# Turning the products of c with the first w_ada columns round, in the prelude of a hybrid attention and retention layer

## The chip, the cores and the metric

The kernel runs on one core of one Trainium2 chip. Its engines are TensorE (PE in the profile, with its weight loads as PEld), VectorE (DVE), ScalarE (ACT), GpSimd (POOL) and SyncE (SP). Each engine works through its own instructions in order, and semaphores hold one engine back until another, or a DMA, has reached a certain point. DMAs are issued from SP, ACT and POOL. The metric is the time of one execution on the device in microseconds (us); lower is better.

## The reference, cut to what matters

All data is float32. The sequence has 512 rows, the model 2048 columns, and there is one layer.

```python
def hybrid_layer(x, c_act, g, w_ada, b_ada, w_in, w_out, dec_f, dec_b):
    mod = c_act @ w_ada + b_ada                      # c_act = silu(c), (1, 2048); w_ada (2048, 6144)
    shift, scale, gate = jnp.split(mod, 3, axis=-1)
    h = rms_norm(x, g) * (1.0 + scale[:, None]) + shift[:, None]
    proj = jnp.einsum('bsd,df->bsf', h, w_in)        # w_in (2048, 7168)
    ...                                              # dilated attention, retention, gates
    out = jnp.einsum('bsf,fd->bsd', y, w_out)
    return x + gate[:, None] * out
```

What the change touches is the first part: for the first 128 model columns (called k = 0 here), the shift and the scale, each a sum over 2048 rows of w_ada, and the first 128 columns of h, which every projection needs.

## The kernel before, in words

**Layout.** The projections want h with the model's columns on the partitions, in 16 pieces of 128 columns by 512 rows. x arrives with its rows on the partitions, in four tiles `xn[0]` to `xn[3]` of 128 rows by 2048 columns (named xt0 to xt3, or xt, in the profile). Each tile is squared and summed (`squares_a` on ACT for the left half, `squares` on DVE for the right half), the factor of the RMS norm is made (`factor`: a small DVE instruction, then a power on POOL), the tile is scaled on DVE (`scaled`), and its 16 blocks of 128 by 128 are transposed by TensorE (`k0_part` for the first block, `turned` for the other 15 in four banks of PSUM) and copied to SBUF (`evacuated`, on ACT or DVE). The first block of each tile stays in PSUM, in `psk` (tiles 0 to 2) and `psk3` (tile 3).

**Shift and scale of k = 0.** They come from two blocks of w_ada, 2048 rows by 128 columns each: `raw0[0]` (shift, raw00 in the order below) and `raw0[1]` (scale, raw01). Each is loaded in two halves of 512 KB (`load0(q, b, i)`: block b, half i), in 512-byte runs. `sums0(b, i)` makes the eight products of half i: before, the 128 by 128 piece of w_ada is the stationary operand and one column of silu(c) (`ct`) the moving one, so the sum lands with one number on each partition, in column b of `psa`. `turn_rows` transposes the row of biases and gains that was loaded from DRAM, and two DVE instructions copy it to `bg`. `shift_scale0` adds the biases and gives `sv` and `av`, and `h0_sum` and `h0_low` make h of k = 0 as a pair: `hh` (rounded) and `hl` (what the rounding left).

**After the prelude.** The projections run over groups of the 16 pieces of h (1, 2, 2, 3, 4 and 4 of them). For the first piece, all 13 first units of w_in (256 columns each) are multiplied with h of k = 0, each as three products (high by high, high by low, low by high). Meanwhile DVE sums the columns of w_ada for the next group (`aacc`, line 214), and splits the weights into high and low parts (`wlo`, line 540).

**What sets the order.** `pin` keeps an instruction at the place where the program text has it on its engine. Instructions without `pin`, among them the two copies of `turn_rows` on DVE, are placed by a scheduler. `warm(n, ps)` issues n products of two constant tiles whose result nobody reads; each product of 128 by 128 floats shows as two rows in the profile. Loads issued from SP and from ACT share eight semaphores, which the build hands out in turn (DMAHW0 to DMAHW7): a ninth load waits, on the engine that issues it, until the earlier load with the same semaphore has landed. On ACT the loads stand ahead of all of its other instructions.

## Time and profile before

| what | us |
|---|---|
| median of 3 runs | 975.18 (973.9 to 975.6) |
| the profiled execution's own time | 976.19 |
| span of its trace | 974.4 |
| PE busy in the span | 952.7 (98%) |
| DVE, ACT, POOL busy | 615.3, 375.4, 14.4 |
| first square of x on ACT (line 308) starts | 5.77 |
| first product with w_ada (line 294) starts | 16.04 |
| first h on ACT (line 364) starts | 37.17 |
| first projection product (line 90) starts | 38.24 |

Times in the trace count from the start of the span. The stretches in the table of windows give, for each engine, its busy time and its number of instructions, then the TensorE clock that was granted (1.00 is full speed), the mean busy share of the DMA engines and the bytes moved. The granted clock has its first record at 8.8 us; the 1.00 shown ahead of that is no measurement. TensorE ends are modelled, so the start-to-start distance of a run of products tells more than the length of one.

### The profile page before, as it was taken

How to read it: one execution, taken by the hardware profiler on the slowest of the kernel's cores; microseconds unless marked ns; L12 is line 12 of the kernel's file. 1: busy time of each engine (PE TensorE's matmuls, PEld its weight loads, DVE VectorE, ACT ScalarE, POOL GpSimd, SP SyncE). 2: the span in 40 equal slices, each digit the busy share in tenths (PEclk: the TensorE clock that was granted, in tenths of full speed). 3: DMA queues.
4: the chain of work that ended last, by engine and by line, in shares of the span. 5: the costliest groups of instructions: out<-in, count | busy, mean ns of one | idle time of the engine just before them, and what ended most of it. 6: DMA issues, size and time to landing. Idle time of an engine off the chain costs nothing.

```text
span 974.4 us, 14375 instructions
## 1 busy us (share of the span) xinstructions
PE 952.7 (98%) x5596; PEld 832.0 (85%) x5596; DVE 615.3 (63%) x1078; ACT 375.4 (39%) x735; POOL 14.4 (1%) x25
## 2 busy tenths in 40 slices
PE   6999899999999999999999999999999999999996
PEld 6887689787988888988998899998899988888896
DVE  4599999957968776664565556745534382535444
ACT  3554425234236554454343242422333372333321
POOL 2000000000000000000000000000000000000001
PEclk8699999999999999999999999999999999999999
DMA  9697889633552122212224625426313158234304
GB/s 330 197 327 234 281 263 325 207 106 109 186 181 78 54 87 65 66 44 87 67 86 143 204 66 184 141 80 202 124 55 98 54 167 284 87 118 141 109 1 173
DMA packets 108947, 141.49 MB, mean 145 GB/s; under 512 B 5656, under 2 KB 78024, under 8 KB 108496
## 3 DMA queue, kind: packets, MB, share of 16 engines
q1 hardware_dynamic: 107056, 135.57, 43.1%
q10 hardware_dynamic: 1728, 4.98, 1.3%
q8 instruction: 44, 0.72, 0.3%
q14 instruction: 23, 0.19, 0.1%
q0 software_dynamic: 96, 0.03, 0.0%
HBM read 136.36 MB, written 4.20 MB: 144 GB/s over the span
## 4 chain that ended last, share of the span: by engine, by line
PE 89%; DMA 4%; DVE 4%; issue 1%; ACT 0%; POOL 0%; SPq 0%; POOLq 0%; DVEq 0%; ACTq 0%
PE pp L92 24%; PE pw L92 15%; PE pp L90 12%; PE po L92 12%; PE pw L90 7%; PE po L90 6%; PE op L92 3%; PE sp L92 2%; DMA graw<-in_w_ada_dram 2%; PE op L90 2%; DMA raw<-in_w_ada_dram 1%; PE tp L774 1%; PE psa L294 1%; PE sp L90 1%; DVE aacc L214 1%
## 5 line engine op out<-in xcount | busy, mean ns | idle before, releaser
L539 ACT CAST whi<-raw 128x512 fp32r<-128x512 f32 (+1 forms) x289 | 175.0, 606 | 428.3 <-PE pp L92 198.1
L540 DVE TENSOR_TENSOR wlo<-raw,whi 128x512 fp32r<-128x512 f32 (+1 forms) x289 | 194.1, 672 | 213.2 <-ACT whi L539 206.6
L90 PE MATMUL pp<-whi,hh 128*128 128x256 f32 x576 | 162.4, 282 | 0.0
L92 PE MATMUL pp<-wlo,hh 128*128 128x256 f32 x576 | 161.8, 281 | 0.3 <-DVE wlo L540 0.3
L92 PE MATMUL pp<-whi,hl 128*128 128x256 f32 x576 | 161.4, 280 | 0.0
L90 PEld LDWEIGHTS pp<-whi,hh 128*128 128x128 f32 x576 | 108.4, 188 | 2.5 <-ACT sc L843 1.7
L92 PEld LDWEIGHTS pp<-wlo,hh 128*128 128x128 f32 x576 | 108.4, 188 | 1.5 <-DVE wlo L540 0.7
L92 PEld LDWEIGHTS pp<-whi,hl 128*128 128x128 f32 x576 | 108.4, 188 | 0.0
L90 PE MATMUL pw<-hh,whi 128*128 128x512 f32 x256 | 103.6, 405 | 3.3 <-DVE acc L946 1.8
L90 PE MATMUL pp<-hh,whi 128*128 128x512 f32 x256 | 101.8, 398 | 0.4 <-DVE kl L674 0.4
L92 PE MATMUL pw<-hh,wlo 128*128 128x512 f32 x256 | 102.1, 400 | 0.0
L92 PE MATMUL pp<-hh,wlo 128*128 128x512 f32 x256 | 101.5, 396 | 0.0
L92 PE MATMUL pw<-hl,whi 128*128 128x512 f32 x256 | 101.5, 397 | 0.0
L92 PE MATMUL pp<-hl,whi 128*128 128x512 f32 x256 | 101.1, 395 | 0.0
L92 PE MATMUL po<-wlo,yh 128*128 128x512 f32 (+1 forms) x252 | 92.6, 367 | 0.0
L90 PE MATMUL po<-whi,yh 128*128 128x512 f32 (+1 forms) x252 | 92.5, 367 | 0.0
L92 PE MATMUL po<-whi,yl 128*128 128x512 f32 (+1 forms) x252 | 92.5, 367 | 0.0
L214 DVE SCALAR_TENSOR_TENSOR aacc<-araw,ct,aacc 128x512 f32<-128x512 f32 (+2 forms) x75 | 76.1, 1015 | 4.1 <-ACT aacc L210 2.7
L946 DVE TENSOR_TENSOR acc<-acc,pw 128x512 f32<-128x512 f32 x100 | 66.9, 683 | 8.2 <-PE pw L92 7.8
L999 DVE SCALAR_TENSOR_TENSOR gacc<-graw,ct,gacc 128x512 f32<-128x512 f32 x60 | 45.0, 750 | 35.1 <-DMA graw<-in_w_ada_dram 34.4
L90 PEld LDWEIGHTS pw<-hh,whi 128*128 128x128 f32 x256 | 48.5, 190 | 18.7 <-DVE acc L946 4.8
L90 PEld LDWEIGHTS pp<-hh,whi 128*128 128x128 f32 x256 | 48.1, 188 | 13.6 <-ACT e L719 0.9
(230 smaller groups left out, 1586.1 us busy)
## 6 DMA issues: line engine op xcount, KB each, us to landing
raw<-in_w_in_dram SPq DMA_DIRECT2D x94, 512.0 KB, 3.6
araw<-in_w_ada_dram SPq DMA_DIRECT2D x48, 512.0 KB, 6.2
graw<-in_w_ada_dram SPq DMA_DIRECT2D x64, 256.0 KB, 2.8
raw<-in_w_out_dram SPq DMA_DIRECT2D x32, 512.0 KB, 3.8
raw<-in_w_in_dram SPq DMA_DIRECT2D x16, 384.0 KB, 4.0
araw<-in_w_ada_dram SPq DMA_DIRECT2D x16, 384.0 KB, 4.2
res<-in_x_dram SPq DMA_DIRECT2D x16, 256.0 KB, 6.0
raw<-in_w_in_dram SPq DMA_DIRECT2D x10, 256.0 KB, 4.1
```

Of the source, the lines that this page charges most:

```text
L90: nc.tensor.matmul(o, lh, rh, start=start, stop=False, skip_group_check=True)
L92: nc.tensor.matmul(o, a, b, start=False, stop=stop and b is (rl if swap else rh), skip_group_check=True)
L214: ins = nc.vector.scalar_tensor_tensor(acc[:, :, :n], rv[:, a], ct[:, kr + a : kr + a + 1], acc[:, :, :n], op0=ALU.mult, op1=ALU.add,)
L294: nc.tensor.matmul(psa[:, b : b + 1], raw0[b][:, a, :], ct[:, a : a + 1], start=a + b == 0, stop=a == NK - 1, skip_group_check=True,)
L539: c1 = nc.scalar.copy(dh, src)
L540: c2 = nc.vector.tensor_tensor(dl, src, f32(dh), op=ALU.subtract)
L774: nc.tensor.transpose(tp_[:, j * P : (j + 1) * P], pt[:, j * P : (j + 1) * P], ident)
L946: nc.vector.tensor_tensor(accs[u][i], accs[u][i], ps[i], op=ALU.add)
L999: nc.vector.scalar_tensor_tensor(st["acc"], raw, ct[:, kr : kr + 1], st["acc"], op0=ALU.mult, op1=ALU.add)
```

## The change

The operands of `sums0` are exchanged: one column of silu(c) is stationary, the 128 by 128 piece of w_ada moves, and the sum is a row of 128 numbers on partition 0 of `psa`. `sums0_turned` copies the two rows to SBUF on ACT and turns them into columns with two small transposes. Tile 1 of x is loaded from ACT's queue and not from SP's, so that the four halves of `raw0` follow directly on half of tile 0 on SP. `h0_sum` is divided: `h0_high` issues the ACT half, and columns 0 to 383 and 384 to 511 are made at different places. The order of the prelude and the counts of warming products are new.

```diff
-WARM = 8, 2, 4, 2
+WARM = 9, 2, 8, 6, 4
...
-    for q, t, a, b in ((nc.scalar, 0, 0, 1024), (nc.sync, 0, 1024, D), (nc.sync, 1, 0, D), (nc.scalar, 2, 0, D), (nc.scalar, 3, 0, D)):
+    for q, t, a, b in ((nc.scalar, 0, 0, 1024), (nc.sync, 0, 1024, D), (nc.scalar, 1, 0, D), (nc.scalar, 2, 0, D), (nc.scalar, 3, 0, D)):
         q.dma_start(xn[t][:, a:b], x2[t * P : (t + 1) * P, a:b])
...
-                    psa[:, b : b + 1], raw0[b][:, a, :], ct[:, a : a + 1],
+                    psa[0:1, b * P : (b + 1) * P], ct[:, a : a + 1], raw0[b][:, a, :],
...
+    def sums0_turned():
+        pin(nc.scalar.copy(row0, psa[0:1, 0 : 2 * P]))
+        for b in range(2):
+            pin(nc.tensor.transpose(psa[:, 256 + b : 257 + b], row0[:, b * P : (b + 1) * P], ident[0:1, 0:1]))
...
+    def h0_high(cols, src):
+        marks["hh"] = pin(nc.scalar.activation(hh[0][:, cols], src, AF.Identity, scale=av[:, 0:1], bias=sv[:, 0:1]))
+
     def h0_sum(cols, src):
-        a, b = av[:, 0:1], sv[:, 0:1]
-        marks["hh"] = pin(nc.scalar.activation(hh[0][:, cols], src, AF.Identity, scale=a, bias=b))
-        pin(nc.vector.tensor_scalar(tmp0[:, cols], src, a, b, op0=ALU.mult, op1=ALU.add))
+        pin(nc.vector.tensor_scalar(tmp0[:, cols], src, av[:, 0:1], sv[:, 0:1], op0=ALU.mult, op1=ALU.add))
...
-    evacuated(0, 0, act)
-    evacuated(0, 1, act)
+    for b in range(4):
+        evacuated(0, b, act)
+    warm(WARM[2], psk3)
+    sums0(0, 0)
+    turn_rows()
     squares_a(1)
     squares(1)
     factor(1)
-    squares_a(2)
-    squares(2)
-    factor(2)
...
+    scaled(1, 1024, D)
+    turned(1, 2)
+    turned(1, 3)
+    sums0(0, 1)
+    squares_a(2)
+    squares(2)
+    factor(2)
+    evacuated(1, 2, act)
+    evacuated(1, 3, act)
+    sums0(1, 1)
     scaled(2, 0, P)
     scaled(2, P, 1024)
+    sums0_turned()
     k0_part(2)
     turned(2, 0)
     turned(2, 1)
+    shift_scale0()
     squares_a(3)
     squares(3)
     factor(3)
-    scaled(1, 1024, D)
+    h0_sum(A, psk[:, A])
+    scaled(3, 0, P)
     scaled(2, 1024, D)
...
+    h0_high(A, psk[:, A])
+    turned(2, 2)
+    warm(WARM[3], ps0)
     k0_part(3)
+    warm(WARM[4], ps0)
+    h0_low(A)
+    marks["conv1"] = [marks["hh"], marks["hl"]]
+    h0_high(B, psk3[:, 0:P])
+    h0_sum(B, psk3[:, 0:P])
+    h0_low(B)
+    turned(2, 3)
```

Where instructions stand, with the semaphores that each waits for. First ACT's queue from the program's start. Before:

```order
L123 DMA xt0_110<-in_x_dram 128x1024
L123 DMA xt2_112<-in_x_dram 128x2048
L123 DMA xt3_113<-in_x_dram 128x2048
L129 DMA raw_122<-in_w_in_dram 128x512
L308 ACT_TABLE_LOAD
L308 ACTIVATE sqa_161,ssx_128<-xt0_110 128x1024 [waits DMAHW0_49]
```

With the change:

```order
L123 DMA xt0_110<-in_x_dram 128x1024
L123 DMA xt1_111<-in_x_dram 128x2048
L123 DMA xt2_112<-in_x_dram 128x2048
L123 DMA xt3_113<-in_x_dram 128x2048 [waits DMAHW0_49]
L129 DMA raw_122<-in_w_in_dram 128x512 [waits DMAHW4_49]
L315 ACT_TABLE_LOAD
L315 ACTIVATE sqa_163,ssx_128<-xt0_110 128x1024
```

ACT now issues five loads, and the last two of them wait: xt3 for the load that had DMAHW0 before it, and raw_122 (the first piece of w_in) for the load that had DMAHW4.

Which load has DMAHW4 is seen on TensorE, with the change, from the eight warming products behind tile 0 on (a product waits for the semaphore of the load it reads):

```order
L378 MATMUL psk3_150<-ident_130,ones_135 128x128 x8
L296 MATMUL psa_147<-raw00_108,ct_141 1x128 [waits DMAHW3_49]
L296 MATMUL psa_147<-raw00_108,ct_141 1x128 x7
L272 MATMUL ps0_149<-ident_130,bg_row_107 128x48 [waits DMASW2_49,DMASW1_49]
L339 MATMUL psk_148<-ident_130,xt1_111 128x128 [waits DMAHW2_49,DVE_49]
L347 MATMUL psx_234<-ident_130,xt1_111 128x128 [waits DVE_49,PE_49,Activation_49]
...
L296 MATMUL psa_147<-raw01_109,ct_141 1x128 [waits DMAHW4_49]
L296 MATMUL psa_147<-raw01_109,ct_141 1x128 x7
L347 MATMUL psx_255<-ident_130,xt1_111 128x128 [waits DVE_49,Activation_49]
```

DMAHW4 belongs to raw01_109, the first half of the scale's block; DMAHW0 (as in ACT's first square before) to the half of tile 0 that ACT loads. The biases' transposes (line 272) stand behind the first eight products on TensorE.

Last, VectorE between tile 0 and tile 1. Before:

```order
L326 TENSOR_SCALAR xt0_110<-xt0_110,rsx_129 128x1024
L313 ISA sqd_203,ssx_128<-xt1_111 128x1024 [waits DMAHW3_49]
L313 ISA ssx_128 128x1
L318 SCALAR_TENSOR_TENSOR ms1_205<-ssx_128 128x1 [waits DVE_49,Activation_49]
L313 ISA sqd_210,ssx_128<-xt2_112 128x1024 [waits DMAHW2_49]
L313 ISA ssx_128 128x1
L273 COPY bg_146<-ps0_149 128x48 [waits PE_49]
```

With the change:

```order
L333 TENSOR_SCALAR xt0_110<-xt0_110,rsx_129 128x1024
L273 COPY bg_146<-ps0_149 128x48 [waits PE_49]
L274 TENSOR_SCALAR bg_146<-bg_146 128x16 [waits DVE_49]
L320 ISA sqd_226,ssx_128<-xt1_111 128x1024 [waits DMAHW2_49]
L320 ISA ssx_128 128x1
L325 SCALAR_TENSOR_TENSOR ms1_228<-ssx_128 128x1 [waits DVE_49,Activation_49]
L333 TENSOR_SCALAR xt1_111<-xt1_111,rsx_129 128x128 [waits Pool_49]
```

The copy of the biases (line 273), which waits for TensorE's line 272, now stands ahead of the squares of tile 1; before, it stood behind the squares of tiles 1 and 2.

## The prediction

> **What bounds the kernel now.** I read the page's first part, then the table of windows over the first 58 us, then the timeline of each engine there. Over the whole span TensorE sets the time, so an edit in the prelude is worth what it moves the start of the projections, counted at full clock.

> ```profile
> PE 952.7 (98%) x5596; PEld 832.0 (85%) x5596; DVE 615.3 (63%) x1078; ACT 375.4 (39%) x735; POOL 14.4 (1%) x25
> ...
> 12.25:16.04 3.79, 0.00 (x0) 0.00 (x1) 3.62 (x11) 1.82 (x4) 2.42 (x2) 0.95 1.09 327
> 16.04:36.89 20.85, 20.85 (x101) 20.55 (x101) 5.91 (x13) 4.97 (x11) 1.28 (x1) 0.50 0.93 285
> 36.89:38.24 1.35, 0.00 (x0) 0.00 (x1) 0.61 (x3) 1.07 (x3) 0.00 (x0) 0.50 0.05 7
> 38.24:43.00 4.76, 4.76 (x13) 3.81 (x14) 4.72 (x10) 2.91 (x7) 0.00 (x0) 0.51 0.22 57
> 43.00:58.00 15.00, 15.00 (x86) 12.93 (x86) 11.70 (x22) 13.07 (x27) 0.00 (x0) 1.00 0.90 283
> ```

> TensorE is idle from 12.25 to 16.04; within that gap the clock falls to half, and it stays there through 20.85 us of unbroken one-column products and transposes, until 42.9, about 4.7 us after dense projection products began at 38.24. So what ends last ahead of the projections is TensorE itself, at half speed, behind a load.

> At full clock two projection products take 0.47 us:

> ```profile
> 45.53 0.47 PE pw L92 x2
> ...
> 40.11 1.05 PE L340 MATMUL psx<-ident,xt 128*128 128x128 f32 x4
> ```

> The 13 instructions of 38.24 to 43.00 are these four transposes and nine products, worth 9 x 0.235 + 4 x 0.13 = 2.6 us at full clock. The present start, at full clock, is thus 43.0 - 2.6 = 40.4. That is the number to beat.

> **The change, part by part.** It removes the half-speed one-column products and would keep the clock up; but it puts two waits into ACT's queue ahead of everything ACT does. Now that queue runs straight through:

> ```profile
> 0.74 1.38 ACTq L123 DMA_DIRECT2D xt<-in_x_dram  x3
> 2.15 1.09 ACTq L129 DMA_DIRECT2D raw<-in_w_in_dram  x1
> 3.27 1.28 ACT L308 ACT_TABLE_LOAD   x1 [3.27 <-issue]
> 5.57 1.23 DVE L313 CUSTOM_DVE_ANT_0 sqd<-xt 128x1024 f32<-128x1024 f32 x1 [4.69 <-DMA xt<-in_x_dram]
> 5.77 1.06 ACT L308 ACTIVATE sqa<-xt 128x1024 f32<-128x1024 f32 x1 [1.23 <-DMA xt<-in_x_dram]
> ```

> The table load follows 0.03 us behind the last DMA issue: they share one order. With the change the fifth issue waits for raw01's first half to land. Queued behind it are the table load, the squares of tile 0 and all copies from PSUM; DVE's factor waits for that square, POOL for the factor, TensorE for the scaled tile. **First term: when does that half land?** With x on ACT's queue (q10) and w_ada's 512-byte runs on SP's (q1) the windows of the DMA show:

> ```profile
> q10 hardware_dynamic: 109, 0.76, 93.2%
> q1 hardware_dynamic: 107, 0.05, 8.6%
> ...
> q1 hardware_dynamic: 1180, 0.60, 118.7%
> ...
> DMA to landing us min/median/max: 15.7/15.7/15.7
> ...
> 16.04 3.57 PE L294 MATMUL psa<-ct,raw 128*128 128x1 f32 x16 [3.83 <-DMA raw<-in_w_ada_dram]
> ```

> The first two are 10 to 12 us, the third 14 to 16, the fourth the one recorded landing among w_ada's four loads. The queues alternate packet by packet, so the queue with small packets gets 0.05 MB while x gets 0.76. Being issued first does not bring w_ada first. After tile 0 (5.57) three tiles of x, 3.15 MB, take 3.15 / 0.38 = 8.3 us, in which w_ada gets 0.2 MB; of the two pieces in question, 1.05 MB, 0.84 remain, at 0.30 MB/us 2.8 us: 16.7. Upper bound: before, the recorded landing fits only the second load, issued at about 2.1, thus 17.8 (the first was in use at 16.04), and the bytes ahead of it are nearly the same now. I take 17.3.

> Restart of ACT: an issue of 0.46 (three in 1.38) to 1.09, the table 1.28, so the first square starts at 19.1 (18.4 to 20.2) instead of 5.77. **Second term: tile 0.**

> ```profile
> 3.67 3.78 PE L372 MATMUL psk<-ident,ones 128*128 128x128 f32 x16 [3.67 <-POOL mln L145]
> 8.62 0.37 PE L332 MATMUL psk<-ident,xt 128*128 128x128 f32 x1
> 8.82 0.97 PE L340 MATMUL psx<-ident,xt 128*128 128x128 f32 x7
> 10.04 1.09 PE L340 MATMUL psx<-ident,xt 128*128 128x128 f32 x8 [0.25 <-DVE xt L326]
> 10.97 1.06 PE L372 MATMUL psk<-ident,ones 128*128 128x128 f32 x8
> 19.72 1.70 PE L340 MATMUL psx<-ident,xt 128*128 128x128 f32 x7
> ```

> The seven transposes came 3.05 us after the square: 22.1. TensorE has by then stood idle since about 8.5, far longer than the 3.8 us that halved its clock, so 15 transposes cost 3.2 (seven took 1.70 at half clock, 0.97 at full): 25.3. Eight warming products, 16 rows, take 3.4 as at the start of the trace: 28.8. Then the first eight products, 16 rows of the warming kind, as the new operands give: 3.4 at half clock, 1.9 at full. With the clock back 4.7 us after dense work began (25.3 + 4.7 = 30.0) they end at 31.2 (30.7 to 32.3).

> **Third term: tile 1, no longer covered.** Its squares and scaling ran from 10.93 to about 15 inside the wait for w_ada. Now DVE's copy of the biases stands ahead of them and waits for a transpose behind those products.

> ```profile
> 13.49 0.20 DVE L273 COPY bg<-ps 128x48 f32<-128x48 f32 x1
> 13.76 0.17 DVE L274 TENSOR_SCALAR bg<-bg 128x16 f32<-128x16 f32 x1
> 10.93 1.23 DVE L313 CUSTOM_DVE_ANT_0 sqd<-xt 128x1024 f32<-128x1024 f32 x1 [0.94 <-DMA xt<-in_x_dram]
> 12.27 0.16 DVE L318 SCALAR_TENSOR_TENSOR ms<-ssx 128x1 f32<-128x1 f32 x1
> 7.27 0.56 POOL L322 TENSOR_TENSOR rsx<-ms,mhalf 128x1 f32<-128x1 f32 x1 [3.57 <-DVE ms L318]
> 14.01 1.83 DVE L326 TENSOR_SCALAR xt<-xt,rsx 128x128 f32<-128x128 f32 x4
> ```

> Bias transpose and copies 0.8: 32.0. Squares to scaling 1.34 + 0.16 + 0.56 and two hand-overs, 2.15; two scalings 0.92: 35.1. TensorE then has 15 transposes (2.0) and 24 products (5.6) at full clock: 42.7. If the cover were still there this term would be nothing.

> **Fourth term: the tail.** The turn back (a PSUM copy on ACT, two transposes of one row, three small adds) is new. Nearest rows: a copy of 256 columns, three in 1.12; the adds from 36.25 to 37.13. I take 1.4, between 1.0 and 2.2: 44.1. Then DVE does tile 3's squares (1.5), the low part's product (0.68) and the scalings of tile 3's first block and tile 2's right half (0.28 + 0.74): 47.3. TensorE follows with four transposes, six and four warming products around one transpose, and four transposes: 20 rows at 0.13 and 9 at 0.13, 3.6. First projection at 50.9, on a full clock.

> ```profile
> 20.82 1.12 ACT L353 COPY xT<-psx 128x256 f32<-128x256 f32 x3 [6.75 <-PE psx L340]
> 36.25 0.15 DVE L301 TENSOR_TENSOR sv<-psa,bg 128x1 f32<-128x1 f32 x1
> 36.98 0.15 DVE L303 TENSOR_TENSOR av<-av,bg 128x1 f32<-128x1 f32 x1
> L365 DVE TENSOR_SCALAR ht<-psk,av,sv 128x384 f32<-128x384 f32 x1 | 0.7, 677 | 0.7 <-ACT hh L364 0.7
> SPq L563 <- DVE av L303: 10.6, 1, 10.6
> ...
> 19.55 6.87 SPq L203 DMA_DIRECT2D araw<-in_w_ada_dram  x6
> 37.09 5.10 SPq L563 DMA_DIRECT2D raw<-in_w_in_dram  x2
> ```

> The two earlier h parts hide under these steps and cost nothing. The pieces of w_ada for the next group wait for the buffers of the squares, which come later now; SP stood 10.6 us with nothing to issue, so that is covered too (up to 1 us if not).

> **Sum:** 50.9 - 40.4 = +10.5 us on the profiled 976.19, so 986.7; the median of the runs is 1.0 lower, so 985.7, and I say **986**.

> [...]

> **Rivals.**

> *The clock falls again (22%).* Between the first products and tile 1 TensorE is idle about 3 us, again about 2.5 between tile 2's transposes. Speaking for it: 3.8 us were enough before, and transposes did not restore it. Price: tile 1's 15 transposes and first products at half, until 4.7 us after these begin, +4.5; a second fall +4 more. 990 to 994.

> *w_ada gets more than packet for packet (8%).* If the queues shared time equally, 1.05 MB would need 7 us behind tile 0, landing near 13 and not 17.3: about 4 us off, 982. The 109 against 107 packets speak against it.

> *ACT is not held (10%): faster.* If the wait sits with the DMA and not with the engine, ACT starts as before, and the change does what it says. The first products start at 16.04 on a live clock: 17.9; biases 18.7; tile 1 21.8; TensorE's 7.6: 29.4; turn 30.8; DVE 34.0; projections at 37.6 instead of 40.4: -2.8, so 972. It is decided on ACT's first square: the eight products wait for 16.04 while tile 0 with its eight warming products is done at 10.97 + 2.1 = 13.1, so there are 2.9 us of slack, and the break-even is a first square near 5.8 + 2.9 + 2.8 = 11.5 us. For it stands only that the trace shows no such wait on ACT; against it the one order of issue and table load above, and SP's 10.6 us, a wait in which nothing behind it was issued. [...]

> **How the numbers follow.** The forecast, held until the landing and the clock back once, has 55% and its own range 982 to 989; the clock's second fall 22%, equal time 8%, ACT free 10%, and 5% for results between 973 and 981 by partial waits. The range 978 to 994 leaves out ACT free and the ends. About 0.2% (2 us) is what this measurement can tell from no change. Faster: nearly all of "ACT free", 9%. Same: 4%. Slower: 87%.

> **What would show it.** In the changed profile: ACT's first square (line 315) near 19 with a gap behind ACT's issue of w_in; granted clock 0.50 at 20 to 30; the first products with w_ada near 29, in rows of 0.12 after the clock's return; h on ACT near 45; the first projection near 51, then a trace like the old one shifted by ten. I am wrong if the first square starts before 11.5, if w_ada's second load lands before 13, or if the projections start before 43.

## The result and the profile after

The changed kernel takes 985.04 us (median; 984.71 to 986.82) against 974.91 for the kernel before beside it: a ratio of 1.0108, 95% interval 1.0091 to 1.0126. It is slower by 1.1%, as forecast (986, 978 to 994). The profiled execution took 985.0 us with a span of 983.2.

First the start of the changed kernel: its timeline up to the first projection product (start in us, duration in us, engine, line, operation, how many; in brackets the idle time before and what ended it).

```profile
17.18 0.33 ACTq L129 DMA_DIRECT2D raw<-in_w_in_dram  x1
17.54 1.28 ACT L315 ACT_TABLE_LOAD   x1 [17.54 <-DMA raw<-in_w_ada_dram]
18.84 1.06 ACT L315 ACTIVATE sqa<-xt 128x1024 f32<-128x1024 f32 x1
...
21.27 0.48 PE L339 MATMUL psk<-ident,xt 128*128 128x128 f32 x1 [12.74 <-DVE xt L333]
...
21.87 3.12 PE L347 MATMUL psx<-ident,xt 128*128 128x128 f32 x15
...
24.82 1.95 PE L378 MATMUL psk<-ident,ones 128*128 128x128 f32 x16
...
26.70 1.91 PE L296 MATMUL psa<-raw,ct 128*1 128x128 f32 x16
...
28.84 0.21 DVE L273 COPY bg<-ps 128x48 f32<-128x48 f32 x1 [5.79 <-PE ps L272]
...
29.16 1.22 DVE L320 CUSTOM_DVE_ANT_0 sqd<-xt 128x1024 f32<-128x1024 f32 x1
...
31.66 0.47 PE L339 MATMUL psk<-ident,xt 128*128 128x128 f32 x1 [2.86 <-DVE xt L333]
...
32.35 1.73 PE L347 MATMUL psx<-ident,xt 128*128 128x128 f32 x7 [0.21 <-DVE xt L333]
...
34.01 3.57 PE L296 MATMUL psa<-raw,ct 128*1 128x128 f32 x16
...
38.82 3.65 PE L296 MATMUL psa<-raw,ct 128*1 128x128 f32 x32
...
46.90 0.63 PE L347 MATMUL psx<-ident,xt 128*128 128x128 f32 x4 [2.67 <-DVE xt L333]
...
50.06 0.48 PE L90 MATMUL pw<-hh,whi 128*128 128x512 f32 x1
```

ACT did nothing until 17.54; what ended its wait was a load of w_ada, right behind its issue of the first piece of w_in (line 129). TensorE stood idle for 12.74 us ahead of tile 0's first transpose, and for 2.86 us more ahead of tile 1's. The same stretches in the table of windows of the changed kernel (busy time and instructions of PE, PEld, DVE, ACT and POOL, then the granted TensorE clock):

```profile
21.09:24.50 3.41, 3.11 (x14) 2.82 (x15) 1.89 (x6) 1.12 (x3) 0.00 (x0) 0.50 1.00 372
24.50:31.33 6.83, 4.30 (x37) 3.48 (x35) 1.69 (x6) 2.14 (x4) 0.55 (x1) 1.00 0.51 153
31.33:38.16 6.83, 6.29 (x27) 4.04 (x28) 3.72 (x8) 2.17 (x5) 0.55 (x1) 0.50 0.19 50
38.16:50.06 11.90, 8.78 (x79) 7.34 (x77) 5.48 (x14) 5.74 (x13) 0.55 (x1) 1.00 0.54 171
```

The clock came back at 24.50, was lost at 31.33 for 6.83 us, and came back at 38.16. The first projection product starts at 50.06 on a full clock. Against the old start counted at full clock, 40.4, that is 9.66 us; from the tenth to the 160th projection product the changed trace is in fact behind the old one by 9.64 to 9.69 us, but for twelve of them (10.1 to 11.2), and up to the 200th by 9.5 to 10.0. So an account of the prelude at full clock gives the shift of the products that follow. Later the changed trace makes up about 1 us (8.4 to 8.7 behind from the 350th product on), and the spans differ by 8.8.

### The profile page after: what moved, and what is told of

The parts are those of the page before. It is cut to its first block, busy times and chain, and to the rows that moved or that the text cites. A ratio compares the mean times of both kernels' runs of the same rounds, so it can differ in the third digit from the quotient of the medians.

```text
span 983.2 us, 14429 instructions
## 1 busy us (share of the span) xinstructions
PE 948.1 (96%) x5624; PEld 824.5 (84%) x5624; DVE 613.9 (62%) x1076; ACT 376.3 (38%) x738; POOL 12.3 (1%) x25
## 4 chain that ended last, share of the span: by engine, by line
PE 87%; DMA 5%; DVE 4%; issue 2%; ACT 1%; POOL 0%; SPq 0%; POOLq 0%; DVEq 0%; ACTq 0%
PE pp L92 24%; PE pw L92 14%; PE pp L90 12%; PE po L92 12%; PE pw L90 7%; PE po L90 6%; PE op L92 3%; PE sp L92 2%; DMA graw<-in_w_ada_dram 2%; DMA raw<-in_w_ada_dram 2%; PE op L90 2%; PE tp L783 1%; DVE aacc L214 1%; PE sp L90 1%; DMA araw<-in_w_ada_dram 1%
## 5 line engine op out<-in xcount | busy, mean ns | idle before, releaser
L92 PE MATMUL pp<-wlo,hh 128*128 128x256 f32 x576 | 161.8, 281 | 0.6 <-DVE wlo L549 0.6
L92 PE MATMUL pp<-whi,hl 128*128 128x256 f32 x576 | 161.3, 280 | 0.0
L92 PEld LDWEIGHTS pp<-wlo,hh 128*128 128x128 f32 x576 | 108.4, 188 | 1.7 <-DVE wlo L549 0.8
L92 PEld LDWEIGHTS pp<-whi,hl 128*128 128x128 f32 x576 | 108.4, 188 | 0.0
L92 PE MATMUL pw<-hh,wlo 128*128 128x512 f32 x256 | 101.4, 397 | 0.0
L92 PE MATMUL pp<-hh,wlo 128*128 128x512 f32 x256 | 101.3, 396 | 0.0
L92 PE MATMUL pw<-hl,whi 128*128 128x512 f32 x256 | 101.1, 395 | 0.0
L92 PE MATMUL pp<-hl,whi 128*128 128x512 f32 x256 | 100.9, 394 | 0.0
L92 PE MATMUL po<-wlo,yh 128*128 128x512 f32 (+1 forms) x252 | 92.6, 367 | 0.0
L92 PE MATMUL po<-whi,yl 128*128 128x512 f32 (+1 forms) x252 | 92.5, 367 | 0.0
```

What stands on the lines that cost most here:

```text
L92: nc.tensor.matmul(o, a, b, start=False, stop=stop and b is (rl if swap else rh), skip_group_check=True)
```

## The experiments

My theory: ACT's queue, held until the first half of the scale's block has landed, makes the loss; what comes behind it (tile 1 uncovered, the clock) sets its size. The rivals: the loss sits in the exchanged operands and their turn back, in the uncovered tile 1, or in the clock alone. No experiment leaves out or changes anything that the reference computes.

**1. Take the wait for w_ada off ACT.** The first piece of w_in is issued from SP, behind the four halves, instead of from ACT.

```diff
     raw_w = raw_tile()
-    nc.scalar.dma_start(raw_w[:, : 2 * UC], wi[0:P, FIRST_W : FIRST_W + 2 * UC])
     load0(nc.sync, 0, 1)
     load0(nc.sync, 1, 1)
+    nc.sync.dma_start(raw_w[:, : 2 * UC], wi[0:P, FIRST_W : FIRST_W + 2 * UC])
```

> The changed kernel with one load moved: the first piece of w_in is issued from SP behind the four halves of the w_ada columns, so ACT no longer waits for a half of them. Theory (the loss is ACT's wait): ACT's first square starts near 7.5 us and not 18.8, the first products start when the first half has landed (15.4), and with the 23.4 us that the changed trace needs from the first products (26.70) to the first projection (50.06), less up to 2.8 us for the second fall of the clock, the projections start at 36 to 39: 971 to 974 us, slightly faster than before. Rival (the longer chain of the new order costs the ten us by itself, the wait hides under it): 982 us or more.

Measured: 974.86 us, 1.000 of the kernel before (0.9978 to 1.0023). The whole loss is gone, and nothing is won. Its timeline:

```profile
6.43 1.28 ACT L315 ACT_TABLE_LOAD   x1 [6.43 <-DMA xt<-in_x_dram]
...
7.73 1.06 ACT L315 ACTIVATE sqa<-xt 128x1024 f32<-128x1024 f32 x1
...
15.69 1.91 PE L296 MATMUL psa<-raw,ct 128*1 128x128 f32 x16
...
20.65 0.48 PE L339 MATMUL psk<-ident,xt 128*128 128x128 f32 x1 [2.87 <-DVE xt L333]
...
22.99 3.57 PE L296 MATMUL psa<-raw,ct 128*1 128x128 f32 x16
...
39.09 0.48 PE L90 MATMUL pw<-hh,whi 128*128 128x512 f32 x1
```

ACT's fourth load of x still waits for tile 0 (until 6.43), but the square starts at 7.73 and not at 18.84, and the projections at 39.09 and not at 50.06: 11.0 us from one line. What is left of the change's cost is seen in the same rows: tile 1 is as uncovered as in the changed kernel (2.87 us idle), and behind it the 16 rows take 3.57 instead of 1.91.

**2. Make the wait alone.** In the kernel before, only tile 1 of x moves to ACT's queue.

```diff
-    for q, t, a, b in ((nc.scalar, 0, 0, 1024), (nc.sync, 0, 1024, D), (nc.sync, 1, 0, D), (nc.scalar, 2, 0, D), (nc.scalar, 3, 0, D)):
+    for q, t, a, b in ((nc.scalar, 0, 0, 1024), (nc.sync, 0, 1024, D), (nc.scalar, 1, 0, D), (nc.scalar, 2, 0, D), (nc.scalar, 3, 0, D)):
```

> The kernel before with one edit of the change alone: tile 1 of x is issued from ACT. That gives ACT the same two waits. Theory (the wait alone makes the loss): first square near 18.8 us, tile 0's transposes end near 25, and from there the 23.4 us that the kernel before needs from 10.97 to 38.24 without its wait for w_ada; less whatever an earlier return of the clock saves: 980 to 986 us. Rival (the loss comes from the new order of products and tiles): within 2 us of the kernel before, 973 to 977 us.

Measured: 984.59 us, 1.008 (1.0056 to 1.0104). The timeline shows the same wait in the old order:

```profile
17.53 0.33 ACTq L129 DMA_DIRECT2D raw<-in_w_in_dram  x1
17.89 1.28 ACT L308 ACT_TABLE_LOAD   x1 [17.89 <-DMA raw<-in_w_ada_dram]
19.19 1.06 ACT L308 ACTIVATE sqa<-xt 128x1024 f32<-128x1024 f32 x1
...
43.81 0.79 PE L90 MATMUL pw<-hh,whi 128*128 128x512 f32 x1 [1.35 <-ACT hh L364]
```

The profiled execution was the fastest of the seven (981.46; the others up to 985.93), so its rows show less of the loss than the median. Most of the change's loss comes with this one word of it, without exchanged operands, new order or turn back. Experiments 1 and 2 together settle the cause: taking the wait away removes the loss, and the wait alone makes most of it.

**3. Exchange the operands alone.** The kernel before, with silu(c) stationary and w_ada moving, and with the turn back, which the old program now issues behind its last product; no load and no order changes. The definition of `sums0_turned` and the columns that `shift_scale0` reads are those of the change, and are not shown again in the diff.

```diff
-                    psa[:, b : b + 1], raw0[b][:, a, :], ct[:, a : a + 1],
+                    psa[0:1, b * P : (b + 1) * P], ct[:, a : a + 1], raw0[b][:, a, :],
...
     marks["conv1"] = [marks[act], marks[dve]]
+    sums0_turned()
     warm(WARM[3], ps0)
```

> The kernel before with the operands of the products exchanged and the two sums turned back, and nothing else of the change: loads, queues, order and warming counts stay. Theory (products that move 128 columns lift the clock gate, one-column products do not): the clock returns at 19 to 23 us and not at 42.9, the stretch from 16.04 on shrinks from 20.9 to about 15 us, plus 1.4 for the turn back; projections at 34 to 36 on a full clock instead of 40.4: 968 to 971 us. Rival (transposes between the products keep the gate down): half clock to the end, the turn back on top: 976 to 977 us.

Measured: 970.01 us, 0.9945 (0.9923 to 0.9967). This part of the change is worth about half a per cent by itself. Its timeline, and one row of its windows behind:

```profile
16.06 3.57 PE L296 MATMUL psa<-raw,ct 128*1 128x128 f32 x16 [3.80 <-DMA raw<-in_w_ada_dram]
...
34.20 0.50 PE L90 MATMUL pw<-hh,whi 128*128 128x512 f32 x1 [1.08 <-ACT hh L371]
```

```profile
35.00:38.41 3.41, 3.41 (x12) 2.67 (x11) 3.41 (x7) 2.23 (x6) 0.00 (x0) 0.50 0.01 3
```

The products wait for the same load as before (16.06 against 16.04), at half clock; but with the operands exchanged the clock comes back at 21.35, while the old one-column products and the transposes among them stayed at 0.50 for 20.85 us. The projections start at 34.20 instead of 38.24, though the clock is lost once more from 35.00 to 38.41.

**4. Keep the clock through that wait.** The same kernel with 18 warming products, not four, ahead of the first load of w_ada; then also six, not two, ahead of the projections. The second of these kernels was measured twice, the second time beside kernels of experiments 6 and 7.

```diff
-WARM = 8, 2, 4, 2
+WARM = 8, 2, 18, 2
```

```diff
-WARM = 8, 2, 18, 2
+WARM = 8, 2, 18, 6
```

> The kernel before with the operands exchanged, and 18 warming products in place of 4 in the gap from 11 us to the first w_ada half at 16.0. Theory (a window without TensorE work halves the clock): no fall at 14.5, the 5.3 us that stood at half clock shrink by 2.6: 967.4 us. Rival (the fall is hidden by DVE, ACT and the landing of the later halves): 970 us.

> As the run before, and 6 warming products in place of 2 while h is made, so that the first projections do not start at half clock. Theory: the fall at 35.0 to 38.4 us that the swapped kernel showed is gone too, another 1.0 to 1.7 us: 966 us. Rival (that fall depends on where the windows lie, and the added products are in the way as often as they help): 967 to 968 us.

> The old order with exchanged operands, 18 and six warming products, once more, so that it stands beside the new order held on one chip: 966.5 to 968.5 us, 0.9945 of the kernel before; the theory that the new order costs by itself wants it 1 to 3 us under that one, the rival within 0.7 us of it.

Measured: 968.3 us, 0.9955 (0.9943 to 0.9968); 967.32 us, 0.9945 (0.9925 to 0.9965); and again 968.13 us, 0.9937 (0.9918 to 0.9957). These beat both kernels. From the second measurement's trace:

```profile
10.93 4.18 PE L379 MATMUL psk<-ident,ones 128*128 128x128 f32 x36
...
16.05 1.91 PE L296 MATMUL psa<-raw,ct 128*1 128x128 f32 x16 [0.75 <-DMA raw<-in_w_ada_dram]
...
31.78 0.50 PE L90 MATMUL pw<-hh,whi 128*128 128x512 f32 x1 [0.18 <-ACT hh L371]
```

The 36 rows fill the idle stretch but for 0.75 us, the first products take 1.91 instead of 3.57, and the projections start at 31.78 on a clock that stays at 1.00 from 16.05 to there. That is 2.4 us ahead of experiment 3, whose clock is also at half for 3.41 us behind the start. The ratios of experiments 3 and 4 overlap, so that the times alone do not show this gain; the rows do. Of the six products ahead of the projections the times show nothing either: 967.32 and 968.13 against 968.3, where 966 was expected and the rival had 967 to 968.

**5. Really load w_ada first.** The change meant its halves to come ahead of most of x. Here tiles 1 to 3 of x stand behind them in the same queue (SP's), so that ACT issues only half of tile 0 and the first piece of w_in.

```diff
-    for q, t, a, b in ((nc.scalar, 0, 0, 1024), (nc.sync, 0, 1024, D), (nc.scalar, 1, 0, D), (nc.scalar, 2, 0, D), (nc.scalar, 3, 0, D)):
+    for q, t, a, b in ((nc.scalar, 0, 0, 1024), (nc.sync, 0, 1024, D)):
         q.dma_start(xn[t][:, a:b], x2[t * P : (t + 1) * P, a:b])
...
     load0(nc.sync, 1, 1)
+    for t in (1, 2, 3):
+        nc.sync.dma_start(xn[t], x2[t * P : (t + 1) * P])
```

> The changed kernel with tiles 1 to 3 of x issued from SP behind the four halves of the w_ada columns; ACT issues only half of tile 0 and the piece of w_in, without a wait. Theory (two queues alternate packet by packet, so only a place behind w_ada on the same queue puts w_ada first): all of w_ada's halves land by 14 us and not 19 to 21, tile 1 at about 16, ACT's first square at 5.8; first products at 13 to 14, tile 1 scaled at 18.9, products done at 26, projections at 34 to 37: 968 to 972 us. Rival (queue order is what counts, whatever the queue): w_ada lands as in the changed kernel, first half at 15.4, and the time is that of the run with w_in on SP, 974 to 975.

Measured: 973.13 us, 0.9995 (0.9978 to 1.0012). What was expected of the loads came true, the gain did not. Its timeline (its lines stand two further down than the changed kernel's):

```profile
8.31 2.69 SPq L133 DMA_DIRECT2D xt<-in_x_dram  x3
...
12.85 1.91 PE L298 MATMUL psa<-raw,ct 128*1 128x128 f32 x16
...
16.30 1.06 ACT L317 ACTIVATE sqa<-xt 128x1024 f32<-128x1024 f32 x1 [4.49 <-DMA xt<-in_x_dram]
...
21.15 3.57 PE L298 MATMUL psa<-raw,ct 128*1 128x128 f32 x16
```

The first products start at 12.85 and do not wait for a load. But SP issues the rest of x only at 8.31, tile 1's square starts at 16.30, behind 4.49 us of waiting for x, and in the hole that this leaves on TensorE the clock falls (0.50 from 18.26 to 25.09, and again from 35.33 on, where eight rows of warming products take 1.91 us against 1.06 in experiment 1, just ahead of the projections, which start at 38.74 and not at 34 to 37). What one load wins the other loses.

**6. Give tile 1 its cover back.** The kernel of experiment 1 with the transpose of the biases ahead of the first products and not behind them; then that kernel with TensorE kept moving where its clock fell (eight warming products instead of two behind silu(c), 22 more behind tile 2's first eight transposes).

```diff
     warm(WARM[2], psk3)
-    sums0(0, 0)
     turn_rows()
+    sums0(0, 0)
```

```diff
-WARM = 9, 2, 8, 6, 4
+WARM = 9, 8, 8, 6, 4
...
     turned(2, 1)
+    warm(22, ps0)
     shift_scale0()
```

> The run with w_in on SP, and the bias transpose put ahead of the first products, so that DVE's copy of the biases no longer holds tile 1 back. Theory (third term: tile 1's squares and scaling lost their cover, 3.4 to 3.9 us): tile 1's squares run at 13.5 to 15, inside the wait for w_ada, its transposes follow the first products at once, 971 us. Rival (the cover is worth nothing, the later tiles set the end): 974 to 975 us, as without this edit.

> The order of bias_first (ACT free, biases ahead of the first products) with TensorE kept moving where its clock fell in that trace: eight instead of two warming products behind silu(c), and 22 more behind tile 2's first eight transposes. Theory (the moved order uncovers tile 1, about 5 us more on TensorE's path between the first and the last products than in the old order, and the clock hides only part of it): first projection at 34 to 35.5 us on a full clock, 968.5 to 970.5 us, above the old order with exchanged operands and a held clock (967.3). Rival (the order costs nothing once ACT is free, only the clock did): first projection near 32, 966.5 to 968, the same as the old order held.

Measured: 971.82 us, 0.9982 (0.9963 to 1.0000); with the clock held 971.3 us, 0.9972 (0.9956 to 0.9988). Timeline of the first of these kernels:

```profile
16.45 1.91 PE L296 MATMUL psa<-raw,ct 128*1 128x128 f32 x16
...
16.56 0.21 DVE L273 COPY bg<-ps 128x48 f32<-128x48 f32 x1 [4.80 <-PE ps L272]
...
19.39 0.33 PE L339 MATMUL psk<-ident,xt 128*128 128x128 f32 x1 [1.03 <-DVE xt L333]
...
36.70 0.48 PE L90 MATMUL pw<-hh,whi 128*128 128x512 f32 x1
```

The idle time ahead of tile 1 falls by 1.84 us, from 2.87 to 1.03, and the projections start 2.4 us earlier than in experiment 1 (36.70 against 39.09); the clock falls at other places in the two traces, which is in that difference too. Tile 1 got only a part of its cover back: its squares were expected at 13.5 to 15, but the biases' transpose stands behind 16 rows of warming products, which ran mostly at half clock here (3.04 us from 13.29 on, against 1.95 for the 16 rows in the changed kernel at 1.00), so the copy waits until 16.56 and the squares start at 16.89. So in the rows the place of the biases is a cost of its own. In the times it is too small to be told apart: the intervals of the two ratios (1.000 and 0.9982) overlap. Of the kernel with the clock held:

```profile
27.47 5.08 PE L378 MATMUL ps<-ident,ones 128*128 128x128 f32 x44
...
29.20 0.95 DVE L333 TENSOR_SCALAR xt<-xt,rsx 128x128 f32<-128x128 f32 x2
...
32.38 0.60 PE L347 MATMUL psx<-ident,xt 128*128 128x128 f32 x4
...
35.52 0.48 PE L90 MATMUL pw<-hh,whi 128*128 128x512 f32 x1
```

The clock stays at 1.00 from 12.00 to the start of the projections at 35.52. But I had sized the 22 products for the gap wrongly: a product is two rows, so 44 rows run until 32.38, while VectorE had the right half of tile 2 ready at 30.15 (29.20 + 0.95). These 2.2 us are mine, not the order's. The start of 35.52 therefore only seems to bear out the 34 to 35.5 expected; without them it would be about 33.3, 1.5 us behind the 31.78 of the old order held. The new order's own cost is thus smaller than the 5 us of TensorE's path that the theory gave it. The times agree: this kernel and the old order held (the second measurement of experiment 4) ran side by side, and all twelve runs of the one (969.01 to 973.65) lie above all six of the other (967.03 to 968.74), 3.2 us apart in the median. Less the 2.2 us, some 1 to 1.5 us are left for the order. That is an estimate; no run without the 2.2 us shows it.

**7. Bridge the changed kernel's idle stretches.** First 12 warming products behind the biases' transpose; then those and 22 behind tile 2's first eight transposes, beside the changed kernel itself.

```diff
     turn_rows()
+    warm(12, ps0)
     squares_a(1)
```

```diff
     turned(2, 1)
+    warm(22, ps0)
     shift_scale0()
```

> The changed kernel with twelve more warming products behind the bias transpose, so that TensorE is not idle from 28.8 to 31.7 us while tile 1 is scaled. Theory (the second fall of the clock costs 2.8 us: 0.75 on seven transposes, 1.6 on eight products, 0.45 on the next transposes): 982 us, granted clock 1.00 throughout 28 to 50. Rival (DVE and ACT set the pace there, so a faster TensorE gains nothing): 985 us with the clock at 1.00.

> The changed kernel itself, on the same chip as the kernel that bridges its two idle stretches. Both theories: 984 to 986 us, 1.010 of the kernel before.

> The changed kernel with both idle stretches of TensorE bridged: 12 warming products behind the biases' transpose and 22 behind tile 2's first eight transposes. Theory (each fall of the clock after 24 us costs 2 to 3 us in about every execution): 982 to 983.2, 2 us under the changed kernel on the same chip, clock at 1.00 from 25 us on. Rival (the falls come in few executions or cost nothing that stays): within 1 us of the changed kernel.

Measured: 984.84 us, 1.0085 (1.0055 to 1.0115); the changed kernel again 987.09 us, 1.0133 (1.0111 to 1.0155); with both bridges 985.58 us, 1.0125 (1.0103 to 1.0146). By the times this is inconclusive. The first bridge's 984.84 is what its rival expected (985); the changed kernel itself came out above the 984 to 986 expected; both bridges gave 1.5 us less than that, between the theory (2) and the rival (within 1). The intervals overlap, and the second bridge is too long here as well, by the same 2.2 us. Single times also differ by what comes after the prelude: from the first projection product to the end, the profiled execution with the first bridge took 932.7 us (span 980.9 less 48.22) and that with both took 936.4 (986.8 less 50.38), at mean granted clocks of 0.990 and 0.991 over the span. The rows of the prelude say more. The changed kernel measured again:

```profile
34.71 2.55 PE L296 MATMUL psa<-raw,ct 128*1 128x128 f32 x16
...
46.29 1.09 PE L347 MATMUL psx<-ident,xt 128*128 128x128 f32 x4 [2.67 <-DVE xt L333]
47.17 2.72 PE L378 MATMUL ps<-ident,ones 128*128 128x128 f32 x12
...
51.09 0.48 PE L90 MATMUL pw<-hh,whi 128*128 128x512 f32 x1
```

The same with the first bridge alone:

```profile
34.12 1.91 PE L296 MATMUL psa<-raw,ct 128*1 128x128 f32 x16
...
45.06 0.63 PE L347 MATMUL psx<-ident,xt 128*128 128x128 f32 x4 [2.67 <-DVE xt L333]
45.53 1.50 PE L378 MATMUL ps<-ident,ones 128*128 128x128 f32 x12
...
48.22 0.48 PE L90 MATMUL pw<-hh,whi 128*128 128x512 f32 x1
```

Bridged, the clock stays at 1.00 from 26.17 on, the same instructions take 1.91, 0.63 and 1.50 instead of 2.55, 1.09 and 2.72, and the projections start 2.9 us earlier, though tile 0's first transpose starts at the same time in both (21.40 and 21.42). So the falls cost about 3 us where they come. How often they come, and so how much of this is in the median, stays open.

## Why the prediction was right, point by point

**The bound and the way of counting** held: TensorE sets the time, and 9.66 us of later start, counted at full clock, became 9.64 to 9.69 us for most of the first 160 products.

**First term, ACT held until raw01's first half lands: right.** Landing 17.18 (forecast 17.3), first square 18.84 (19.1). The packets of the two queues are nearly as many also in the changed kernel, 110 against 109 from 10 to 12 us:

```profile
q10 hardware_dynamic: 110, 0.77, 94.2%
q1 hardware_dynamic: 109, 0.06, 9.8%
```

With x behind w_ada in one queue (experiment 5) the first products needed no wait at 12.85.

**Second term, tile 0: mis-sized by 2.6 us.** The transposes started at 21.87 (forecast 22.1) and took 2.95 to the next instruction (3.2). The step that failed is "with the clock back 4.7 us after dense work began", which counted only products, not transposes, as dense work: the clock came back at 24.50, not 30.0, while TensorE had done nothing but transposes for 3.2 us, behind 12.74 us of doing nothing at all. So the warming products took 1.88, not 3.4, and the first products ended at 28.54, not 31.2.

**Third term, tile 1 uncovered: right in kind, mis-sized by 2.4 us the other way.** The wait of VectorE's squares for the biases is in the rows (28.84, then 29.16), TensorE was idle for 2.86 us, and with the biases moved ahead (experiment 6), which gave back a part of the cover, 1.84 us of the like were gone. But "TensorE then has 15 transposes and 24 products at full clock" failed: the idle stretch cost the clock from 31.33 to 38.16. The seven transposes took 1.73 instead of 0.96, the products 3.57 instead of 1.91, the eight transposes 1.38 instead of 1.09: 2.7 us. That is the first half of the rival "the clock falls again" (22%), at 2.7 instead of the 4.5 us that it was priced at; the second half, a second fall, was seen when the kernel was measured again, with 987.09.

**Fourth term, the tail: right.** 7.6 us from the last product (42.47) to the first projection, forecast 8.2. The turn back took 1.3 us to the last add (1.4). One sum in this term is slightly off: 29 rows at 0.13 make 3.8 us and not 3.6. They took 3.2 (46.90 to 50.06).

The two errors nearly cancel (2.6 less, 2.4 more, 0.6 less in the tail), which is why 50.06 lies so near to 50.9. The total was better than its terms.

**The rivals.** "Equal time" for w_ada is out by the packets. "ACT is not held" is out by ACT's row at 17.54. What the change would then do was also mis-sized: 972 was forecast and experiment 1, which frees ACT of the wait for w_ada, gives 974.86, with no gain. That sum had the square at 5.8 and the clock held; in experiment 1 it is 7.73, since the fourth load of x waits too, and the clock falls from 20.40 to 27.23.

## What to carry to other kernels

An engine that issues loads and computes paid here with its computing for a load that had to wait (ACT's first square at 18.84 behind w_ada's landing, at 7.73 in experiment 1 behind tile 0's): count the loads of all queues that share the semaphores, in the order in which the build hands these out, before a load is moved onto such a queue. When a change has several parts, measure each alone: here the exchange of operands was worth 0.55% by itself, the rest of the change (its order, its other loads, its warming counts) gave that back even with ACT free of the wait for w_ada (1.000), and that wait made it a loss of 1.1%. A wait ahead of TensorE can cost twice, once as idle time and once as half clock behind it (in experiment 3, 3.80 us idle and then 3.57 instead of 1.91 us for 16 rows), so products that nobody reads are worth issuing into it (in experiment 4 the 16 rows took 1.91 behind 36 rows of them), but only as many as the gap holds (the 44 rows of experiment 6 ran 2.2 us past it).

## What the runs showed of the hardware that was not expected

```profile
27.02:30.44 3.42, 3.42 (x31) 3.25 (x30) 2.86 (x8) 0.97 (x4) 1.16 (x2) 1.00 0.98 331
30.44:37.26 6.82, 6.82 (x35) 6.82 (x34) 3.11 (x7) 3.32 (x8) 1.28 (x1) 0.50 0.92 291
37.26:40.68 3.42, 3.42 (x35) 3.42 (x36) 0.99 (x3) 0.78 (x2) 0.00 (x0) 1.00 0.02 4
```

  That it is the columns is argued from these traces; no run varied their number by itself.
